# Both parts of a stationary float32r operand stored column by column in turn, in two transformer blocks on one core

## The chip, the cores and the metric

One Trainium2 chip, of which one core runs the kernel. The metric is device microseconds of one execution, the median of the runs shown. All inputs lie in the device's memory (DRAM) and are read from there in every execution.

## The reference, cut to what matters

Two transformer blocks of two layers each work one after the other on S = 256 tokens of width D = 1024 in float32. A layer of the first block is a mixer and a PEER layer; a layer of the second is a mixer (attention beside a Fourier mix) and a SwiGLU.

```python
# block 1, per layer
h = _modulate(x, sh1, sc1)
mix = _hybrid_mixer(h, ...)                 # projections, attention, conv, stick breaking, @ w_o
x = _layer_norm(ALPHA * x + (1 + g1) * mix, ...)
h = _modulate(x, sh2, sc2)
ffn = _peer(h, wq, sub_k1, sub_k2, U, V)    # per head the best 16 of 128 x 128 experts
x = _layer_norm(ALPHA * x + (1 + g2) * ffn, ...)
# _peer, per token: act = gelu(U[e] . h);  out = sum over e of g_e * act_e * V[e]
# block 2, per layer
p = h @ w_in                                # q, k, v, u
mix = concat([attention(q, k, v), fourier_mix(u)]) @ w_out
ffn = (silu(h @ w_gate) * (h @ w_up)) @ w_down   # hidden width 2816
```

The context stream of the second block has the same mixer and FFN in its first layer. What a float32 product needs of precision decides how it is made here (next section).

## The kernel before

**A product in three.** [...] So `split(dst_h, dst_l, src)` takes a float32 tile apart: ACT copies it, rounded, to `dst_h` (L261, "hi"), and DVE subtracts that from the source into `dst_l` (L263, "lo"). `mm3(o, lh, ll, rh, rl)` adds three products into one PSUM tile: lh x rh (L286), lh x rl (L287), ll x rh (L288). In each the first operand is the stationary one, which a weight load (LDWEIGHTS, shown as PEld) brings into the array, 128 columns of it; the second one is moving, and streams through, 256 or 512 columns. A load overlaps the matmul before it.

**Weights.** `wtile` starts the transfer of a raw weight tile of 512 KB on SP's queue (`raw_tile`, L256, five buffers), and splits it in two cuts. Each cut has a tile `wh` and a tile `wl`, two tags of the pool `ring` with five buffers (NHL) of 2048 B per partition each, so that hi and lo of one cut lie five buffers, 10,240 B, apart.

**Two kinds of products.**
- `gemm_t` (L290): the weight is stationary, [128 x 128] per k step; the activations (`hh`, `hl`, turned, 256 tokens) are the moving side. So are made the mixer projections of block 1 (`turned`: `sq`, `sk`, `cb`, `cc`, `ch`, L627), the PEER queries (`pwq`, L934), the expert inputs (`pact`, L958, the U stage), the projections of block 2 (`project`: `pw`) and the FFN's gate and up (`pwg`, `pwu`). Each weight tile is 8 k steps x 3 = 24 products of 256 columns.
- The products back to width 1024: the activations are stationary, 128 tokens by 128 channels, and the weights are the moving side, 512 columns. These are the expert outputs (`acc` with `WHL`, the V stage), the output projections of block 2 (`po`: stationary `mix`, or the FFN's `a` and `b`), and w_o of block 1 (`pm`: stationary `catH`, `catL`). For `pm` the split weights are `wok`, and for the last part of one `po` `kw`: both hold hi and lo in one tile [128, 2, 2, 512], 2048 B apart. `pn` (w1n) and `psc` have other stationaries.

**Stages of a PEER layer.** Queries and top-k with the first experts of the U stage beside them (layer 0: to some 415 us), the U stage with one-hot gate products `pG` (to 640 us), then the V stage (to 1005 us): there DVE multiplies the experts' activations by the gates (`Ws<-Ws,Gt`, L1024, which reads `Gt` with a step of 64 words), ACT and DVE split the product into `WHL`, and `acc` sums over 16,384 experts.

**Order.** A scheduler sorts the instructions of each engine from the program's order and its own costs; `Filler` generators put pieces of other work (top-k, gates, modulation products `adap` and `adac`) between the products, and `issue_after` pins some. One load of the kernel reads its stationary operand with a step of two words: `py` (L1321), where `uT` is read at every second token. The products of `adac` (L407) have a single moving column.

## Time and profile before

| | |
|---|---|
| median of 3 runs | 2874.16 us (2872.48 to 2876.75) |
| profiled execution | 2868.95 us, its span 2866.5 us |
| mean granted TensorE clock | 0.995 |
| TensorE busy / weight loads | 2802.3 us (98%) / 2436.2 us (85%) |
| DVE / ACT busy | 2204.3 us (77%) / 1673.2 us (58%) |
| read from and written to DRAM | 600.06 MB / 34.64 MB |

The span is the time from the first to the last instruction of the profiled execution; 2.45 us of that execution lie outside it. PE is TensorE's matmul, PEld its weight load, which runs beside matmuls. A matmul is pipelined: its own duration (279 ns for 256 columns, for instance) is longer than the distance from its start to the next start, so the busy share says only that something is in flight; the pace is read from counts in a stretch or from consecutive starts. [...] In names such as `pact<-hh,wh` the written tile stands left of the arrow, the read ones right.

### The profile page before, as it was taken

How to read it: one execution, taken by the hardware profiler on the slowest of the kernel's cores; microseconds unless marked ns; L12 is line 12 of the kernel's file. 1: busy time of each engine (PE TensorE's matmuls, PEld its weight loads, DVE VectorE, ACT ScalarE, POOL GpSimd, SP SyncE). 2: the span in 40 equal slices, each digit the busy share in tenths (PEclk: the TensorE clock that was granted, in tenths of full speed). 3: DMA queues.
4: the chain of work that ended last, by engine and by line, in shares of the span. 5: the costliest groups of instructions: out<-in, count | busy, mean ns of one | idle time of the engine just before them, and what ended most of it. 6: DMA issues, size and time to landing. Idle time of an engine off the chain costs nothing.

```text
span 2866.5 us, 53009 instructions
## 1 busy us (share of the span) xinstructions
PE 2802.3 (98%) x19114; PEld 2436.2 (85%) x19114; DVE 2204.3 (77%) x5110; ACT 1673.2 (58%) x3459; POOL 39.5 (1%) x50
## 2 busy tenths in 40 slices
PE   7999999999999999999999999999999999998999
PEld 4569999998888766899999888878769999887997
DVE  4469998987789767799888777888769766577565
ACT  3445568985555444555889655555556555566554
POOL 0000000000000000000000000000000000000000
PEclk9999999999999999999999999999999999999999
DMA  9775766667789867577666777976647665652454
GB/s 320 234 278 197 236 228 199 195 207 246 236 269 312 291 237 251 188 237 231 211 202 196 236 238 233 331 262 216 224 158 265 218 202 187 203 180 68 159 190 155
DMA packets 188112, 639.74 MB, mean 223 GB/s; under 512 B 22708, under 2 KB 24116, under 8 KB 187208
## 3 DMA queue, kind: packets, MB, share of 16 engines
q1 hardware_dynamic: 179208, 604.90, 63.9%
q10 hardware_dynamic: 8640, 31.46, 2.7%
q8 instruction: 149, 2.44, 0.3%
q14 instruction: 115, 0.94, 0.1%
HBM read 600.06 MB, written 34.64 MB: 221 GB/s over the span
## 4 chain that ended last, share of the span: by engine, by line
PE 92%; DVE 3%; DMA 2%; ACT 2%; issue 0%; POOL 0%; SPq 0%; DVEq 0%; POOLq 0%; ACTq 0%
PE pact L286 9%; PE pact L288 8%; PE pact L287 8%; PE acc L286 8%; PE acc L288 8%; PE acc L287 8%; PE po L286 3%; PE po L288 3%; PE po L287 3%; PE adap L340 2%; PE pwu L288 2%; PE pwu L287 2%; PE pwu L286 2%; PE pwg L286 2%; PE pwg L288 2%; PE pwg L287 2%
## 5 line engine op out<-in xcount | busy, mean ns | idle before, releaser
L261 ACT ACTIVATE wh<-raw 128x512 fp32r<-128x512 f32 (+1 forms) x1636 | 1010.0, 627 | 826.6 <-PE acc L288 289.8
L263 DVE TENSOR_TENSOR wl<-raw,wh 128x512 fp32r<-128x512 f32 (+1 forms) x1636 | 1094.2, 684 | 391.6 <-ACT wh L261 384.5
L286 PE MATMUL pact<-hh,wh 128*128 128x256 f32 x2048 | 583.0, 285 | 0.0
L288 PE MATMUL pact<-hh,wl 128*128 128x256 f32 x2048 | 572.3, 279 | 0.2 <-DVE wl L263 0.2
L287 PE MATMUL pact<-hl,wh 128*128 128x256 f32 x2048 | 571.4, 279 | 0.0
L286 PE MATMUL acc<-wh,WHL 128*128 128x512 f32 x1024 | 404.5, 396 | 1.2 <-ACT WHL L261 1.2
L288 PE MATMUL acc<-wh,WHL 128*128 128x512 f32 x1024 | 405.2, 396 | 0.0
L287 PE MATMUL acc<-wl,WHL 128*128 128x512 f32 x1024 | 405.1, 396 | 0.0
L287 PEld LDWEIGHTS pact<-hl,wh 128*128 128x128 f32 x2048 | 385.5, 188 | 0.0
L286 PEld LDWEIGHTS pact<-hh,wh 128*128 128x128 f32 x2048 | 385.3, 188 | 0.0
L288 PEld LDWEIGHTS pact<-hh,wl 128*128 128x128 f32 x2048 | 384.9, 188 | 0.4 <-DVE wl L263 0.4
L286 PEld LDWEIGHTS acc<-wh,WHL 128*128 128x128 f32 x1024 | 192.4, 188 | 50.2 <-ACT WHL L261 3.3
L287 PEld LDWEIGHTS acc<-wl,WHL 128*128 128x128 f32 x1024 | 192.4, 188 | 47.2 <-DVE WHL L263 0.9
L288 PEld LDWEIGHTS acc<-wh,WHL 128*128 128x128 f32 x1024 | 192.4, 188 | 47.1 <-DVE WHL L263 0.9
L985 ACT ACTIVATE hot<-hot,idxT 128x128 f16<-128x128 f16 x512 | 173.9, 401 | 1.3 <-DVE hot L984 1.2
L984 DVE TENSOR_SCALAR hot<-hot,idxT 128x128 f16<-128x128 f16 x512 | 158.6, 310 | 20.1 <-PE pG L986 19.8
L288 PE MATMUL pwu<-f,wl 128*128 128x256 f32 x512 | 143.1, 280 | 1.6 <-DVE wl L263 1.6
L286 PE MATMUL pwg<-f,wh 128*128 128x256 f32 x512 | 143.2, 280 | 0.0
L288 PE MATMUL pwg<-f,wl 128*128 128x256 f32 x512 | 143.0, 279 | 0.0
L287 PE MATMUL pwg<-f,wh 128*128 128x256 f32 x512 | 142.9, 279 | 0.0
L286 PE MATMUL pwu<-f,wh 128*128 128x256 f32 x512 | 142.9, 279 | 0.0
L287 PE MATMUL pwu<-f,wh 128*128 128x256 f32 x512 | 142.9, 279 | 0.0
(475 smaller groups left out, 5077.8 us busy)
## 6 DMA issues: line engine op xcount, KB each, us to landing
raw<-in_U_dram SPq DMA_DIRECT2D x256, 512.0 KB, 3.5
raw<-in_V_dram SPq DMA_DIRECT2D x256, 512.0 KB, 4.3
adaw<-in_ada_dram SPq DMA_DIRECT2D x192, 512.0 KB, 6.1
raw<-in_wg_dram SPq DMA_DIRECT2D x66, 512.0 KB, 3.5
raw<-in_wu_dram SPq DMA_DIRECT2D x66, 512.0 KB, 3.8
raw<-in_wd_dram SPq DMA_DIRECT2D x66, 512.0 KB, 3.3
spill<-gab ACTq DMA_DIRECT2D x60, 512.0 KB, 5.0
Ws<-spill SPq DMA_DIRECT2D x120, 256.0 KB, 3.9
```

The costliest lines, as they stand in the source:

```text
L261: SC.activation(dst_h, src, AF.Copy)
L263: return V.tensor_tensor(dst_l, src, dst_h, op=OP.subtract).ins
L286: T.matmul(o, lh, rh, start=first, stop=False)
L287: T.matmul(o, lh, rl, start=False, stop=False)
L288: T.matmul(o, ll, rh, start=False, stop=last)
L340: T.matmul(ps[32 * q:32 * q + 32, :], cvec(blk, k), r[h][:, 512 * (q % 2):512 * (q % 2) + 512], start=k == 0, stop=k == KB - 1, skip_group ...
L984: V.tensor_scalar(B, iota16, i2, g, op0=OP.is_equal, op1=OP.mult)
L985: SC.activation(B2, B, AF.Copy, scale=share)
```

## The change

Four things are done to layouts; the products and their order in the program stay as they are written.

- `pair` makes one tile with a last dimension of two, and returns its two views, so that a column's hi word and lo word are neighbours and each part is read and written with a step of two words (8 B). The stationary activations use it: `cat`, `WHL`, `mix`, `a`, `b`.
- `wtile(..., paired=True)` does the same for the weights of all `gemm_t` calls: tile `whl` [128, cut, 128, 2]. A load of 128 columns then reaches over 1024 B per partition in place of 512 B.
- The weights that are the moving side (V, `wo2`, `wd`) and `w1n` become one tile `whl` [128, 2, ...]: hi and lo, each contiguous, 2048 B apart, as in `wok` and `kw`.
- `turn_in` puts its `hh` and `hl` into one tile. Moving operands are contiguous as before. `ring` has one tag of five buffers of twice the size, so its size stays.

ACT writes, and DVE reads and writes, with a step of two words wherever a pair is split.

```diff
--- before.py
+++ after.py
@@ -256,6 +256,12 @@
         SP.dma_start(r, src)
         return r
 
+    def pair(p, n, cols, nm, tag=None):
+
+
+        t = p.tile([128, n, cols, 2], F32R, name=nm, tag=tag or nm)
+        return t[:, :, :, 0], t[:, :, :, 1]
+
     def split(dst_h, dst_l, src):
         with after(PIN.get("act")):
             SC.activation(dst_h, src, AF.Copy)
@@ -268,7 +274,7 @@
     def after(ins):
         return tc.issue_after(ins) if ins else ExitStack()
 
-    def wtile(src, shape, cuts=None, keep=None):
+    def wtile(src, shape, cuts=None, keep=None, paired=False):
 
 
         r = raw_tile(src, shape)
@@ -276,7 +282,12 @@
         c0 = 0
         for cut in cuts or [shape[0] // 2] * 2:
             sh = [cut] + shape[1:]
-            h, lo = [(keep or ring).tile([128] + sh, F32R, name=nm, tag=nm, bufs=4 if keep else NHL) for nm in ("wh", "wl")]
+            if paired:
+                t = ring.tile([128, cut, sh[1], 2], F32R, name="whl", tag="whl", bufs=NHL)
+                h, lo = t[:, :, :, 0], t[:, :, :, 1]
+            else:
+                t = (keep or ring).tile([128, 2] + sh, F32R, name="whl", tag="whl", bufs=4 if keep else NHL)
+                h, lo = t[:, 0], t[:, 1]
             LAST[0] = split(h, lo, r[:, c0:c0 + cut])
             parts.append((h, lo))
             c0 += cut
@@ -574,8 +585,7 @@
             SP.dma_start(cw, a["small1"][l])
             sh, sc = mod_cols(1, l, 0), mod_cols(1, l, 1)
             sth = ExitStack()
-            catH = p.tile([128, KB, S], F32R, name="catH")
-            catL = p.tile([128, KB, S], F32R, name="catL")
+            catH, catL = pair(p, KB, S, "cat")
             sbv = p.tile([128, 2, 256], F32, name="sbv")
             qln = p.tile([128, 2, 384], F32, name="qln")
             krn = p.tile([128, 2, 128], F32, name="krn")
@@ -624,7 +634,7 @@
                 i = 2 * order.index(nm)
                 ps = bank([128, 2, S], nm, "m")
                 for j in range(2):
-                    gemm_t(ps[:, j], wtile(a["w1t"][l, i + j], [KB, 128]), hh, hl, 0, S)
+                    gemm_t(ps[:, j], wtile(a["w1t"][l, i + j], [KB, 128], paired=True), hh, hl, 0, S)
                     ex.run(pace)
                 if nm in proj:
                     SC.activation(proj[nm], ps, AF.Copy)
@@ -931,7 +941,7 @@
                         pq = early[blk][1]
                     else:
                         pq = bank([128, S], "pwq", "a")
-                        gemm_t(pq, wtile(a["wq"][l, blk], [KB, 128]), hh, hl, 0, S)
+                        gemm_t(pq, wtile(a["wq"][l, blk], [KB, 128], paired=True), hh, hl, 0, S)
                     q = p.tile([128, S], F32, name="pqT", bufs=3)
                     SC.activation(q, pq, AF.Copy)
                     if prev:
@@ -955,7 +965,7 @@
                 ga = gab[:, j // 4 % 2]
                 ps = bank([128, 2, S], "pact", "a")
                 for c in range(2):
-                    gemm_t(ps[:, c], wtile(a["U"][l, j + c], [KB, 128]), hh, hl, 0, S)
+                    gemm_t(ps[:, c], wtile(a["U"][l, j + c], [KB, 128], paired=True), hh, hl, 0, S)
                     fl.run(budget / 2)
                 SC.activation(ga[:, j % 4:j % 4 + 2], ps, AF.Gelu)
                 if j % 4 == 2 and j < 120:
@@ -1004,7 +1014,7 @@
         stb.enter_context(banks(f"pb{l}", acc=2, m=3))
         acc = [bank([128, 2, 512], f"acc{tb}", "acc") for tb in range(2)]
         Ws = pa.tile([128, 4, 2, S], F32, name="Ws", tag="ha")
-        WHL = pa.tile([128, 2, 2, 2, S], F32R, name="WHL", tag="hb")
+        WHL = pair(pa, 4, S, "WHL", "hb")
         stl, stk = ExitStack(), ExitStack()
         held = {}
         last = None
@@ -1022,7 +1032,8 @@
                 spilled(j + 6)
             with tc.issue_after(last) if last else ExitStack():
                 V.tensor_tensor(W, W, Gt[j // 64][:, :, j % 64:j % 64 + 2].rearrange("p t j -> p j t"), op=OP.mult)
-            WH, WL = WHL[:, j // 2 % 2, 0], WHL[:, j // 2 % 2, 1]
+            b = 2 * (j // 2 % 2)
+            WH, WL = [part[:, b:b + 2] for part in WHL]
             last = split(WH, WL, W)
             late = j in order[-2:] and l == 0
             v = [wtile(a["V"][l, :, j + c, :], [1024], keep=kp if late and j == order[-1] else None) for c in range(2)]
@@ -1171,7 +1182,8 @@
                         tail(tb)
 
         def turn_in(p, s, cs, nm, bufs, px=None):
-            hh, hl = [p.tile([128, KB, S], F32R, name=f"{nm}{i}{s}", tag=f"{nm}{i}") for i in range(2)]
+            hp = p.tile([128, 2, KB, S], F32R, name=f"{nm}{s}", tag=nm)
+            hh, hl = hp[:, 0], hp[:, 1]
             for tb in range(2):
                 make_hT(px or p, xs[s][:, tb], "rms", cs[0], cs[1], hh, hl, 128 * tb, "m", bufs)
             return hh, hl
@@ -1192,7 +1204,7 @@
         mixT = {}
 
         def mix_tiles(s):
-            mixT[s] = [pm.tile([128, KB, S], F32R, name=f"mix{s}{i}", tag=f"mix{s}{i}") for i in range(2)]
+            mixT[s] = pair(pm, KB, S, f"mix{s}")
 
         stu = ExitStack()
         pq = stu.enter_context(pool(f"q{l}"))
@@ -1218,7 +1230,7 @@
             def project(b, hs):
 
 
-                w = wtile(a["w2t"][l, b], [KB, 128])
+                w = wtile(a["w2t"][l, b], [KB, 128], paired=True)
                 for s, (hh, hl) in hs.items():
                     ps = bank([128, 256], "pw2", "m")
                     gemm_t(ps, w, hh, hl, 0, S)
@@ -1454,7 +1466,7 @@
 
 
         fa1 = stp.enter_context(pool(f"ffa{l}"))
-        act[order[0]] = [fa1.tile([128, FB, S], F32R, name=f"a{i}") for i in range(2)]
+        act[order[0]] = pair(fa1, FB, S, "a")
         if both:
             fh0 = stp.enter_context(pool(f"ffg{l}"))
             sta = ExitStack()
@@ -1466,14 +1478,14 @@
                 ex.run()
                 stv.close()
                 fa0 = sta.enter_context(pool(f"ffb{l}", side="right"))
-                act[0] = [fa0.tile([128, FB, S], F32R, name=f"b{i}") for i in range(2)]
+                act[0] = pair(fa0, FB, S, "b")
             for f in range(FB):
                 if s:
                     ex.run(18.0 / (FB - 2))
                 pgu = [e[1] for e in early[2 * f:2 * f + 2]] if s == 0 else []
                 for nm in ("wg", "wu")[len(pgu):]:
                     pgu.append(bank([128, S], "p" + nm, "m"))
-                    gemm_t(pgu[-1], wtile(a[nm][l, f], [KB, 128]), *H[s], 0, S)
+                    gemm_t(pgu[-1], wtile(a[nm][l, f], [KB, 128], paired=True), *H[s], 0, S)
                 pg, pu = pgu
                 sg = fx.tile([128, S], F32, name="sg", bufs=2)
                 SC.activation(sg, pg, AF.Silu)
```

The number of instructions on each engine is the same before and after. Their order moves at few places. ACT, at the end of a block of queries in layer 0 (`wh`, `whl` are splits of weights, `pqT` copies of finished queries, `s` the scores' copies out of PSUM), the kernel before:

```order
L261 ACTIVATE wh<-raw 128x512 x2
L936 ACTIVATE pqT<-pwq 128x256
L261 ACTIVATE wh<-raw 128x512 x2
L936 ACTIVATE pqT<-pwq 128x256
L948 ACTIVATE s_1721<-pss_1795 128x512
L948 ACTIVATE s_1722<-pss_1796 128x512
L261 ACTIVATE wh<-raw 128x512 x2
L936 ACTIVATE pqT<-pwq 128x256
```

The two splits of the last weight stand behind both score copies. And the changed kernel, ACT at the same place:

```order
L267 ACTIVATE whl<-raw 128x512 x2
L946 ACTIVATE pqT<-pwq 128x256
L267 ACTIVATE whl<-raw 128x512 x2
L946 ACTIVATE pqT<-pwq 128x256
L267 ACTIVATE whl<-raw 128x512
L958 ACTIVATE s_1684<-pss_1756 128x512
L958 ACTIVATE s_1685<-pss_1757 128x512
L267 ACTIVATE whl<-raw 128x512
L946 ACTIVATE pqT<-pwq 128x256
```

Of the last weight before the next `pqT` one split now stands ahead of the two score copies and one behind them; before, both stood behind.

TensorE at the same place (`pss` are the score products, `pwq` the queries), the kernel before:

```order
L288 MATMUL pwq<-hh,wl 128x256
L921 MATMUL pss_1795<-pk,pqT 128x128
L921 MATMUL pss_1796<-pk,pqT 128x128
L286 MATMUL pwq<-hh,wh 128x256
L287 MATMUL pwq<-hl,wh 128x256
L288 MATMUL pwq<-hh,wl 128x256
L286 MATMUL pwq<-hh,wh 128x256
L921 MATMUL pss_1795<-pk,pqT 128x128
L921 MATMUL pss_1796<-pk,pqT 128x128
L287 MATMUL pwq<-hl,wh 128x256
L288 MATMUL pwq<-hh,wl 128x256
```

Four query products stand between the two pairs of score products. And the changed kernel, TensorE:

```order
L299 MATMUL pwq<-hh,whl 128x256
L931 MATMUL pss_1756<-pk,pqT 128x128
L931 MATMUL pss_1757<-pk,pqT 128x128
L297 MATMUL pwq<-hh,whl 128x256
L931 MATMUL pss_1756<-pk,pqT 128x128
L931 MATMUL pss_1757<-pk,pqT 128x128
L298 MATMUL pwq<-hl,whl 128x256
L299 MATMUL pwq<-hh,whl 128x256
L297 MATMUL pwq<-hh,whl 128x256
L298 MATMUL pwq<-hl,whl 128x256
```

The second pair of score products has moved ahead of a k step of the queries by three `pwq` products; all else stands as it stood.

## Rows read from the trace of the kernel before

**Rows 1.** The page: busy time of each engine, and the chain that ended last by engine.
```profile
PE 2802.3 (98%) x19114; PEld 2436.2 (85%) x19114; DVE 2204.3 (77%) x5110; ACT 1673.2 (58%) x3459; POOL 39.5 (1%) x50
PE 92%; DVE 3%; DMA 2%; ACT 2%; issue 0%; POOL 0%; SPq 0%; DVEq 0%; POOLq 0%; ACTq 0%
```

**Rows 2.** Windows: from:to, us, busy (x count) of PE, PEld, DVE, ACT, POOL, PEclk, DMA.
```profile
300.00:400.00 100.00, 100.00 (x860) 100.00 (x859) 94.64 (x238) 56.13 (x92) 0.00 (x0) 1.00 0.71 235
700.00:900.00 200.00, 200.00 (x858) 161.00 (x858) 160.96 (x226) 105.03 (x179) 0.00 (x0) 1.00 0.80 265
2654.50:2664.00 9.50, 9.50 (x44) 7.86 (x43) 4.09 (x7) 2.45 (x6) 0.55 (x1) 1.00 0.38 132
2200.00:2240.00 40.00, 40.00 (x345) 40.00 (x344) 33.88 (x52) 21.96 (x43) 0.00 (x0) 1.00 0.84 293
```

**Rows 3.** Groups by shape, TensorE's matmuls: busy us, mean ns of one | idle before.
```profile
L286 PE MATMUL pact<-hh,wh 128*128 128x256 f32 x2048 | 583.0, 285 | 0.0
...
L288 PE MATMUL acc<-wh,WHL 128*128 128x512 f32 x1024 | 405.2, 396 | 0.0
...
L288 PE MATMUL pwu<-f,wl 128*128 128x256 f32 x512 | 143.1, 280 | 1.6 <-DVE wl L263 1.6
...
L288 PE MATMUL po<-wh,a 128*128 128x512 f32 x176 | 69.6, 395 | 0.0
...
L288 PE MATMUL po<-wh,b 128*128 128x512 f32 x88 | 34.8, 396 | 0.0
...
L288 PE MATMUL po<-wh,mix 128*128 128x512 f32 x80 | 31.7, 396 | 0.0
...
L288 PE MATMUL po<-kw,mix 128*128 128x512 f32 x16 | 6.2, 389 | 0.0
```

**Rows 4.** Timeline, TensorE: start us, duration us, of `sq` in layer 1's mixer.
```profile
1043.80 0.28 PE L286 MATMUL sq<-hh,wh 128*128 128x256 f32 x1
...
1045.80 0.28 PE L288 MATMUL sq<-hh,wl 128*128 128x256 f32 x1
```

**Rows 5.** Timeline, TensorE: `cc` in the same mixer, 50 us later.
```profile
1094.96 0.28 PE L286 MATMUL cc<-hh,wh 128*128 128x256 f32 x1
...
1097.11 0.28 PE L287 MATMUL cc<-hl,wh 128*128 128x256 f32 x1
```

**Rows 6.** Timeline, TensorE: the projection of the last mixer with kept weights `kw`.
```profile
2657.79 0.39 PE L287 MATMUL po<-kw,mix 128*128 128x512 f32 x1
...
2659.38 0.39 PE L288 MATMUL po<-kw,mix 128*128 128x512 f32 x1
```

**Rows 7.** Groups by shape, TensorE's weight loads of 128 columns.
```profile
L286 PEld LDWEIGHTS pact<-hh,wh 128*128 128x128 f32 x2048 | 385.3, 188 | 0.0
...
L1333 PEld LDWEIGHTS pf<-k,Y 128*128 128x128 f32 x96 | 11.1, 192 | 0.3 <-ACT es L1366 0.2
...
L1321 PEld LDWEIGHTS py<-M,uT 128*128 128x128 f32 x48 | 9.0, 196 | 2.7 <-ACT PT L1385 1.7 <-ACT P L1370 0.2
```

**Rows 8.** Timeline, TensorE: 16 products with one moving column in a row.
```profile
938.99 1.84 PE L407 MATMUL adac<-k,adacc 128*128 128x1 f32 x16
```

**Rows 9.** Line 407: ns of its matmuls, lowest, median, highest; first and last start us.
```profile
L407 PE MATMUL adac<-k,adacc x48: 165/250/250, 939.0 to 2275.9; 128*128 128x1 f32 x48
```

**Rows 10.** Groups by shape, ACT: the split's first half.
```profile
L261 ACT ACTIVATE wh<-raw 128x512 fp32r<-128x512 f32 x1604 | 995.3, 630 | 797.6 <-PE acc L288 284.5 <-PE pact L287 139.5 <-PE po L288 89.6
```

**Rows 11.** Groups by shape, DVE: the split's second half, and the gating product.
```profile
L263 DVE TENSOR_TENSOR wl<-raw,wh 128x512 fp32r<-128x512 f32 x1604 | 1078.2, 687 | 382.2 <-ACT wh L261 375.8 <-PE sk L287 1.4 <-PE pw L288 1.4
...
L1024 DVE TENSOR_TENSOR Ws<-Ws,Gt 128x512 f32<-128x512 f32 x120 | 131.4, 1095 | 0.0
```

**Rows 12.** Windows of layer 0's stages: U with top-k, U with gates, V.
```profile
262.00:415.00 153.00, 152.82 (x1310) 152.62 (x1309) 145.42 (x392) 87.17 (x142) 0.00 (x0) 1.00 0.73 239
415.00:640.00 225.00, 225.00 (x2148) 222.09 (x2148) 199.53 (x684) 197.81 (x523) 0.00 (x0) 1.00 0.62 200
640.00:1005.00 365.00, 364.40 (x1571) 291.35 (x1573) 289.79 (x411) 189.23 (x323) 0.17 (x1) 1.00 0.81 269
```


## The prediction

> **What bounds the kernel now.** I read the page's totals first, then the chain, then stretches in which nothing but one kind of product runs. TensorE is busy for 98% of the span, and the chain that ended last lies on it for 92%, spread over the three lines of `mm3` [rows 1]. So the time is a number of matmuls times the distance from one start to the next, and the question is what sets that distance. The stretches answer it [rows 2]. [...] From 700 to 900 us, in the V stage, 858 of 512 columns: 233.1 ns. The FFN's gate and up products, 2200 to 2240 us, give 345 in 40 us, again 116 ns. TensorE shows no idle time there, so no wait sets this pace. [...]
>
> The pace is not the same everywhere. The products of `sq` at 1043.80 to 1045.80 us make 17 steps in 2.00 us, 117.6 ns [rows 4]; those of `cc` at 1094.96 to 1097.11 us, the same code with the same moving tiles, make 19 steps in 2.15 us, 113.2 ns [rows 5]. Among the 512-column products `po<-kw,mix` is the exception: from 2654.5 to 2664 us there are 44 in 9.50 us [rows 2], a pace that its starts from 2657.79 to 2659.38 us, 7 steps in 1.59, give exactly [rows 6], and one lasts 389 ns, while `po<-wh,mix` with the same stationary tile lasts 396 and the other products of the kind 395 to 396 [rows 3]. What differs is where the moving parts lie: `kw` keeps hi and lo in one tile, 2048 B apart, the ring's `wh` and `wl` are two tags 10,240 B apart. So there are two paces, 233.3 and 226.7, 116.7 and 113.3, and an identical product can run at either, depending on how its operands meet in the memory. That is what this change touches.
>
> **The change part by part.** No instruction is added or removed; matmuls, loads, splits and transfers keep their number, and the few places where the order changes are single splits and half k steps. At the end of a query block ACT now takes one split ahead of the two copies of `s`, which come later by it, and TensorE makes the second pair of `pss` three products, 0.35 us, earlier. I cost the order at nothing: who waits for `s` is the top-k on DVE, and TensorE has expert products queued that need none of it; without that cover it would be one split, 0.63 us [rows 10], at some 16 block ends, at most 10 us.
>
> *Merged halves for the 512-column products.* V, wo2 and wd tiles become one tile with hi and lo 2048 B apart, which is the layout of `kw`. `acc` has 3 x 1024 products, `po` from the ring 3 x (176 + 88 + 80) [rows 3], together 4104. The nearest row is `kw` itself: 226.7 in place of 233.3, 6.67 ns x 4104 = **-27 us**. [...] I take -27, the row that has this moving layout.
>
> *Stationary operands read at every second word.* All `gemm_t` weights, 256-column products: `pact` 3 x 2048 and `pwg`, `pwu` 3 x 1024 [rows 3], 9216, and by the loops of the code another 1,872 (`pwq` 624, `project` 768, mixer 480), together 11,088. Two things can happen. The load can become longer. One load in the kernel before already reads every second word: `py<-M,uT`, 196 ns, against 192 for `pf<-k,Y` right behind it and 188 for `pact` [rows 7]. So +4 to +8 ns. What a load costs when it alone sets the pace is seen at `adac`, with one moving column: 16 in 1.84 us [rows 8], of which the last lasts between 0.165 and 0.250 [rows 9], so 106 to 112 ns each; since 112 is below 116.7, loads are just hidden today, with some 5 ns to spare. If the 4 to 8 ns are a delay at its start, they vanish in the overlap; if they are pace, loads come every 116 to 120 ns and are level with the matmuls or above. Or the load can get out of the moving stream's way, and the products fall to the short pace that `cc` shows: 3.33 ns x 11,088 = **-37 us**. The ends are (120 - 116.7) x 11,088 = +37 us (the 8 ns whole as pace) and -52 us (down to 112, where today's loads would bind). I take -37: the short pace is a row of this very product, and the load's extra 4 ns, if it is delay, stays below the 113.3.
>
> *The splits write and read every second word.* Each of ACT's copies writes with a step of 8 B, each of DVE's subtractions reads one operand and writes one with that step. No row shows an engine doing this. DVE's split of a weight takes 687 ns, ACT's 630 [rows 10, 11]; the nearest row with a stepped operand is `Ws<-Ws,Gt`, which reads with a step of 64 words and takes 1095 ns, 408 more than a contiguous one. I take 687 unchanged, since a step of two is nearest to none; the bounds are 687 and 1095. What covers it: in the U stage with top-k, 262 to 415 us, DVE is busy 145.42 of 153 us [rows 12]. 1310 matmuls / 24 per weight x 2 halves = 109 splits, so 7.58 / 109 = 70 ns each are free: up to 757 ns the stride is free, above it DVE sets the end. From 415 to 640 us it has 25.5 us over some 136 splits, 187 ns each. In the V stage, 640 to 1005 us, only one split in five is strided, and DVE has 75 us. The shorter pace itself takes 1310 x 3.33 = 4.4 us of the 7.58, so it just fits.
>
> [...] The row shows a stepped load 4 ns longer than the plain one beside it [rows 7]. [...]
>
> **Sum.** -27 - 37 = -64 us. The profiled execution is 2868.95 us (span 2866.5 and 2.45 outside it), 5.2 us below the median of 2874.16; against it the sum is 2805, against the median **2810 us**, which is my forecast.
>
> **Rivals.**
> 1. *Only the merged tiles act* (the pace hangs on the moving layout, and `gemm_t`'s moving tiles `hh`, `hl` of block 1 stay as they were): -27, 2847. For: in `po` only the moving side differs between the two paces. Against: `sq` and `cc` differ with no layout changed at all. Chance 0.13.
> 2. [...] Chance 0.12. [...]
> 3. *Nothing moves.* [...] Chance 0.17.
> 4. *The stepped load becomes the bound* of the 256-column products. It decides from 116.7 ns, a load longer by 5 in pace; at 118.5 to 120 it costs 1.8 to 3.3 ns x 11,088 = +20 to +37: 2894 to 2911. Where the merged tiles act too it is 27 less, and the change comes out slower only from some 119.5. For: loads fill the U stage without a gap (100.00 of 100 us) [rows 2], with 5 to 11 ns between their own pace and the matmuls'. Against: the single stepped row is only 4 ns longer. Chance 0.20. Slower.
> 5. *DVE becomes the bound* in the U stage, from 757 ns per split. At 1095: 109 x 0.408 - 7.6 = 37 us, and 136 x 0.408 - 25.5 = 30, each in two layers: +134, up to 3008; at 850, 109 x 0.163 - 7.6 = 10, twice: +20. Chance 0.08. Slower.
>
> **How the numbers follow.** The forecast itself, both kinds at the short pace, has 0.30. Cases that are faster by more than 0.2% (5.7 us, about what a measurement of this kernel can tell from no change): 0.30 + 0.13 + 0.12 = 0.55. Same: 0.17. Slower: 0.20 + 0.08 = 0.28. The faster cases alone span 2740 to 2850. The range that should hold 8 in 10 takes in these, "nothing moves" and most of rival 4 and leaves out its far end and most of rival 5, some 0.14 together: 2740 to 2905.
>
> **What would show it.** Short pace: 300 to 400 us holds 882 matmuls in place of 860, `acc` lasts about 389 ns and its starts lie 227 ns apart. Merged only: `acc` falls, `pact` stays at 116.7. [...] Load bound: `pact` loads without a gap and starts above 116.7, while `po` and `acc` keep or better theirs. DVE: the group of weight splits above 757 ns and TensorE waiting for it in the U stage. The sum is wrong if the `pact` loads come back longer by more than 5 ns per start, or if the pace of `acc` does not follow that of `kw`.

## The result and the profile after

The changed kernel takes 2912.34 us in the median of 4 runs (2906.18 to 2914.77), the kernel before 2875.45 us (4 runs too, one more than above): a ratio of 1.0126, 95% interval 1.0107 to 1.0145, so it is 1.3% slower. The forecast was 2810, the range ended at 2905.

The page of the changed kernel, busy time of each engine and the chain by engine, to stand beside [rows 1]; then its windows, with the columns of [rows 2] (us; busy and count of PE, PEld, DVE, ACT, POOL; PEclk, the granted clock, 1.00 its full speed; DMA share; GB/s):

```profile
span 2904.4 us, 52798 instructions
PE 2843.4 (98%) x19114; PEld 2514.4 (87%) x19114; DVE 2212.3 (76%) x5110; ACT 1714.6 (59%) x3459; POOL 38.4 (1%) x50
PE 92%; DMA 3%; DVE 3%; ACT 2%; issue 0%; SPq 0%; POOL 0%; DVEq 0%; POOLq 0%; ACTq 0%
```

```profile
300.00:400.00 100.00, 100.00 (x829) 100.00 (x829) 92.68 (x235) 58.13 (x90) 0.00 (x0) 1.00 0.70 223
700.00:900.00 200.00, 200.00 (x864) 168.74 (x863) 160.11 (x226) 106.45 (x180) 0.00 (x0) 1.00 0.80 262
262.00:415.00 153.00, 153.00 (x1267) 153.00 (x1267) 143.23 (x379) 87.63 (x135) 0.00 (x0) 1.00 0.71 230
```

TensorE is still busy without a gap, at the same granted clock of 1.00, and gets through fewer products: 829 of 256 columns in 100 us where 860 stood, 120.6 ns each in place of 116.3. The V stage is a little faster: 864 in 200 us, 231.5 ns in place of 233.1. DVE isn't the bound: TensorE and its loads wait for nothing in the U stage (153.00 of 153 us each), while DVE is busy for 143.23 us there, 145.42 before [rows 12]. Groups by shape of the changed kernel, weight loads, the splits on ACT and DVE, and three products:

```profile
L298 PEld LDWEIGHTS pact<-hl,whl 128*128 128x128 f32 x2048 | 404.2, 197 | 0.0
...
L299 PEld LDWEIGHTS acc<-whl,WHL 128*128 128x128 f32 x1024 | 200.6, 196 | 37.8 <-DVE WHL L269 0.8
...
L1333 PEld LDWEIGHTS py<-M,uT 128*128 128x128 f32 x48 | 9.0, 196 | 2.6 <-ACT PT L1397 1.7 <-ACT P L1382 0.2
```

```profile
L267 ACT ACTIVATE whl<-raw 128x512 fp32r<-128x512 f32 x1604 | 1034.2, 657 | 666.2 <-PE acc L299 279.8 <-PE pact L299 103.5 <-PE po L299 88.6
```

```profile
L269 DVE TENSOR_TENSOR whl<-raw,whl 128x512 fp32r<-128x512 f32 x1604 | 1080.4, 689 | 406.7 <-ACT whl L267 403.3
```

```profile
L299 PE MATMUL acc<-whl,WHL 128*128 128x512 f32 x1024 | 404.0, 395 | 0.0
...
L299 PE MATMUL pm<-wok,cat 128*128 128x512 f32 x64 | 25.2, 394 | 0.0
...
L299 PE MATMUL po<-kw,mix 128*128 128x512 f32 x16 | 6.3, 395 | 0.0
```

The loads of `pact` and `acc` now last as long as that of `py`, 196 to 197 ns against 188 [rows 7]. The splits' groups mix stepped and contiguous weights: DVE 689 ns (687 before), ACT 657 (630). From 415 to 640 us all weights are stepped; there ACT's copies take 672 ns in place of 626 (before, then after), DVE's subtractions 688 in place of 686:

```profile
L261 ACT ACTIVATE wh<-raw 128x512 fp32r<-128x512 f32 x137 | 82.4, 626 | 10.2 <-PE pact L287 9.4 <-ACT wh L261 0.8
```

```profile
L267 ACT ACTIVATE whl<-raw 128x512 fp32r<-128x512 f32 x132 | 83.1, 672 | 3.4 <-DVE whl L269 1.4 <-PE pact L299 1.0 <-PE pG L996 0.7
```

And `po<-kw,mix`, the row that my first term rested on, has gone the wrong way, from 389 ns to 395. By the two windows the sum is +4.3 ns x 11,088 = +48 us for the 256-column products and -1.6 x 4104 = -7 for the others, +41 together, near the 37.9 by which the spans differ. A window's count takes in the products under way at its start and a few of other kinds. By the starts of all neighbouring products of a trace (steps across another product or a missing record left out) `pact` goes from 116.9 to 120.7 ns and `acc` from 233.3 to 232.1: +3.8 x 11,088 = +42 and -1.2 x 4104 = -5, together +37.

### The profile page after: what moved, and what is told of

It reads as the page before. It is cut to its first block, busy times and chain, and to the rows that moved or that the text cites. A ratio compares the mean times of both kernels' runs of the same rounds, so it can differ in the third digit from the quotient of the medians.

```text
span 2904.4 us, 52798 instructions
## 1 busy us (share of the span) xinstructions
PE 2843.4 (98%) x19114; PEld 2514.4 (87%) x19114; DVE 2212.3 (76%) x5110; ACT 1714.6 (59%) x3459; POOL 38.4 (1%) x50
## 4 chain that ended last, share of the span: by engine, by line
PE 92%; DMA 3%; DVE 3%; ACT 2%; issue 0%; SPq 0%; POOL 0%; DVEq 0%; POOLq 0%; ACTq 0%
PE pact L297 9%; PE pact L298 9%; PE pact L299 8%; PE acc L297 8%; PE acc L299 8%; PE acc L298 8%; PE adap L351 3%; PE po L297 3%; PE po L298 2%; PE po L299 2%; PE pwu L299 2%; PE pwu L298 2%; PE pwu L297 2%; PE pwg L297 2%; PE pwg L299 2%; PE pwg L298 2%
## 5 line engine op out<-in xcount | busy, mean ns | idle before, releaser
L267 ACT ACTIVATE whl<-raw 128x512 fp32r<-128x512 f32 (+1 forms) x1636 | 1048.8, 654 | 694.7 <-PE acc L299 285.4
L269 DVE TENSOR_TENSOR whl<-raw,whl 128x512 fp32r<-128x512 f32 (+1 forms) x1636 | 1096.5, 685 | 415.9 <-ACT whl L267 411.9
L297 PE MATMUL pact<-hh,whl 128*128 128x256 f32 x2048 | 594.3, 290 | 0.0
L298 PE MATMUL pact<-hl,whl 128*128 128x256 f32 x2048 | 584.5, 285 | 0.0
L299 PE MATMUL pact<-hh,whl 128*128 128x256 f32 x2048 | 581.9, 284 | 0.0
L297 PE MATMUL acc<-whl,WHL 128*128 128x512 f32 x1024 | 403.4, 395 | 1.3 <-ACT WHL L267 1.3
L298 PEld LDWEIGHTS pact<-hl,whl 128*128 128x128 f32 x2048 | 404.2, 197 | 0.0
L298 PE MATMUL acc<-whl,WHL 128*128 128x512 f32 x1024 | 404.0, 395 | 0.0
L299 PE MATMUL acc<-whl,WHL 128*128 128x512 f32 x1024 | 404.0, 395 | 0.0
L297 PEld LDWEIGHTS pact<-hh,whl 128*128 128x128 f32 x2048 | 403.7, 197 | 0.0
L299 PEld LDWEIGHTS pact<-hh,whl 128*128 128x128 f32 x2048 | 403.4, 197 | 0.0
L297 PEld LDWEIGHTS acc<-whl,WHL 128*128 128x128 f32 x1024 | 200.5, 196 | 41.1 <-ACT WHL L267 3.4
L299 PEld LDWEIGHTS acc<-whl,WHL 128*128 128x128 f32 x1024 | 200.6, 196 | 37.8 <-DVE WHL L269 0.8
L298 PEld LDWEIGHTS acc<-whl,WHL 128*128 128x128 f32 x1024 | 200.6, 196 | 37.6 <-DVE WHL L269 0.9
L299 PE MATMUL pwu<-f,whl 128*128 128x256 f32 x512 | 145.8, 285 | 1.5 <-DVE whl L269 1.5
L297 PE MATMUL pwg<-f,whl 128*128 128x256 f32 x512 | 145.9, 285 | 0.0
L299 PE MATMUL pwg<-f,whl 128*128 128x256 f32 x512 | 145.6, 284 | 0.0
L298 PE MATMUL pwg<-f,whl 128*128 128x256 f32 x512 | 145.6, 284 | 0.0
L298 PE MATMUL pwu<-f,whl 128*128 128x256 f32 x512 | 145.5, 284 | 0.0
L297 PE MATMUL pwu<-f,whl 128*128 128x256 f32 x512 | 145.5, 284 | 0.0
```

The costliest lines, as they stand in the source:

```text
L267: SC.activation(dst_h, src, AF.Copy)
L269: return V.tensor_tensor(dst_l, src, dst_h, op=OP.subtract).ins
L297: T.matmul(o, lh, rh, start=first, stop=False)
L298: T.matmul(o, lh, rl, start=False, stop=False)
L299: T.matmul(o, ll, rh, start=False, stop=last)
```

## The experiments

Two questions were open: which part of the change makes the 256-column products slower, and what sets the two paces that the kernel before shows. The theory (A) is that a load at a step of two words is itself too slow to hide. Its rivals are (B) the stepped splits on ACT and DVE and (C) the merged tiles.

### The change taken apart: weights, activations, merging alone

e1, against the changed kernel: the activations are contiguous, the weights of `gemm_t` stay stepped.

```diff
     def pair(p, n, cols, nm, tag=None):
-        t = p.tile([128, n, cols, 2], F32R, name=nm, tag=tag or nm)
-        return t[:, :, :, 0], t[:, :, :, 1]
+        t = p.tile([128, 2, n, cols], F32R, name=nm, tag=tag or nm)
+        return t[:, 0], t[:, 1]
```

> Only the weights of the 256-column products alternate hi and lo; the stationary activations hold their two halves one behind the other, 2048 B or more apart. Theory A, the stepped load is itself the slower one: pact loads 197 ns, 829 products from 300 to 400 us as in the changed kernel, 4.0 ns x 11,088 = +44 us against the kernel before, less what the merged 512-column tiles bring (0 to 27). Theory B, the time goes to the splits' stepped writes and reads on ACT and DVE: the same time as the changed kernel, but by waits of TensorE for splits. Rival C, the merged tiles cost it and not the step: no more than +10 us here with loads of 188 ns.

e2 leaves `pair` as it is and takes `paired=True` away from all five calls of `wtile`:

```diff
-    gemm_t(..., wtile(a["U"][l, j + c], [KB, 128], paired=True), hh, hl, 0, S)
+    gemm_t(..., wtile(a["U"][l, j + c], [KB, 128]), hh, hl, 0, S)
```

> Only the stationary activations of the 512-column products alternate hi and lo; the weights of the 256-column products hold two contiguous halves in one tile. Theory A: acc loads 196 ns, but hidden under 232 ns: acc starts 231 to 233 ns apart, pact back at 116.7 with loads of 188, in all -5 to 0 us against the kernel before; and pm with kept w_o goes from 227 to 233 ns as in the changed kernel. If instead the step is a help to 512-column products, acc comes down to 227 or less: -27 us.

e3 does both, so that only the merging of hi and lo into one tile is left.

> Nothing alternates; only hi and lo halves are in one tile, contiguous, 2048 B apart (wtile, turn_in) or one half apart (activations). If the short pace of kw and w_o belongs to the moving layout with plain loads: acc and po from the ring at 226.7 ns, -27 us against the kernel before, and pact at 116.7 or 113.3. If that pace is a matter of address or phase: the time of the kernel before within 6 us.

Measured against the kernel before: e1 2912.28 us, ratio 1.0137 (1.0119 to 1.0154); e2 2871.81, 0.9999 (0.9989 to 1.0009); e3 2875.07, 1.0009 (0.9998 to 1.0019). The whole loss comes with the stepped weights. The first three fences are windows of e1, e2 and e3, U stage and V stage; the last two are the load of `pact` and the split on ACT in e2:

```profile
300.00:400.00 100.00, 100.00 (x830) 100.00 (x829) 92.11 (x231) 57.76 (x89) 0.00 (x0) 1.00 0.70 227
700.00:900.00 200.00, 200.00 (x858) 160.99 (x857) 158.12 (x224) 105.24 (x179) 0.00 (x0) 1.00 0.79 259
```

```profile
300.00:400.00 100.00, 100.00 (x859) 100.00 (x859) 95.35 (x245) 56.24 (x92) 0.00 (x0) 1.00 0.72 232
700.00:900.00 200.00, 200.00 (x863) 168.44 (x863) 160.83 (x227) 106.88 (x180) 0.00 (x0) 1.00 0.81 265
```

```profile
300.00:400.00 100.00, 100.00 (x852) 100.00 (x851) 94.58 (x236) 55.46 (x92) 0.00 (x0) 1.00 0.73 229
700.00:900.00 200.00, 199.51 (x855) 160.14 (x854) 157.04 (x221) 104.59 (x178) 0.00 (x0) 1.00 0.80 258
```

```profile
L298 PEld LDWEIGHTS pact<-hl,whl 128*128 128x128 f32 x2048 | 385.7, 188 | 0.0
```

```profile
L267 ACT ACTIVATE whl<-raw 128x512 fp32r<-128x512 f32 x1604 | 990.2, 629 | 667.2 <-PE acc L299 277.8 <-PE pact L299 105.8 <-PE po L299 89.0
```

e1 has the 830 products of the changed kernel in 100 us, e2 the 859 of the kernel before; e3 has 852 in this window, but 117.1 ns for `pact` by all starts, as e2 has 116.9. The stepped activations bring the small gain of the V stage (863 in 200 us); with `pm` and `kw` slower it is worth some 3 us by the paces, at the edge of what e2's interval can tell. C falls with e3; the merged layout does not give `acc` the pace of `kw` either: `acc` stays at 233 ns there (855 in 200 us), with nothing stepped. e1 alone can't tell A from B, since weights that are read at a step are also split at one. The trace of the changed kernel can: between two starts of `pact` lie 120.7 ns on average where no split of a weight runs on ACT or DVE (1022 steps), and 120.8 where one runs on both for nearly all of the time (542 steps). In the kernel before these are 117.1 and 116.8. The loss is there whether a split runs beside the products or not, and TensorE has no idle time in the U stage; B falls.

### Loads without splits beside them

The probes leave the reference's work out: they load a few weights and run chains of products on a core whose other engines are idle, so only the pace of a chain counts. The first has this core, in which `one`, `two`, `four` are stationary tiles with a step of 1, 2, 4 words, `m256` and `mnear`, `mfar` moving tiles of 256 and 512 columns, the latter two with hi and lo 2048 or 10,240 B apart; the single loads behind the chains belong to plain float32 products:

```python
for i in range(n):
    mm3(ps[:, :cols], *st[i % len(st)], *mv[i % len(mv)], i == 0, i == n - 1)
```

> A probe without the reference's work: it loads some weights, splits nothing, and runs chains of 96 float32r products in triples as in mm3, one chain behind another, with no other engine at work, and 48 float32 products with one moving column for stationary steps of 1, 2 and 4 words. Theory A: the chain qone (256 columns, contiguous) at about 116.7 ns from start to start, qtwo (step 2) at about 120.6, qfour (step 4) at 120.6 or more; the one-column products 112 at step 1 and 117 to 121 at step 2, more at step 4. Theory B (writes beside it): qone and qtwo the same. For 512 columns: rnearone 226.7 and rfarone 233.3 if the moving layout sets the pace; both the same if it does not; rneartwo and rfartwo about 232 as in the changed kernel.

Timeline of this probe (start us, duration us), first and last rows of stretches of four chains: 85 steps of `qfour`, 86 of `rnearone` and 85 of `rneartwo`, and 84 of `qtwo` ahead of them:

```profile
52.13 0.28 PE L286 MATMUL qtwo<-hh,ctwo 128*128 128x256 f32 x1
...
62.21 0.28 PE L286 MATMUL qtwo<-hh,ctwo 128*128 128x256 f32 x1
...
63.65 0.39 PE L286 MATMUL qfour<-hh,cfour 128*128 128x256 f32 x1
...
83.48 0.40 PE L287 MATMUL qfour<-hl,cfour 128*128 128x256 f32 x1
...
107.83 0.39 PE L286 MATMUL rnearone<-vhl,cone 128*128 128x512 f32 x1
...
127.33 0.39 PE L288 MATMUL rnearone<-vhl,cone 128*128 128x512 f32 x1
...
152.00 0.39 PE L286 MATMUL rneartwo<-vhl,ctwo 128*128 128x512 f32 x1
...
171.83 0.39 PE L287 MATMUL rneartwo<-vhl,ctwo 128*128 128x512 f32 x1
```

`qtwo` makes 10.08 / 84 = 120.0 ns with no split anywhere: near the pace of the changed kernel. `qfour` needs 19.83 / 85 = 233 ns, twice that. With 512 columns a contiguous load allows 19.50 / 86 = 226.7, a stepped one 233.3, so there the step can cost too. `rfarone` and `rnearone` had the same pace, 226.7: how far apart the moving halves lie made no difference there. But `qone`, contiguous, also ran at 120.0, not at the 116.9 that `pact` has in the kernel before. That was the outcome named for B, so this probe by itself does not speak for A; and the step was not the only thing that sets the pace. What differed, by the addresses that the allocator gives, is the place of the operands: in the probe both start at the same place within 64 bytes, in the kernel before `pact` and `acc` have them 32 bytes apart, and `kw` and `wok`, the fast ones, 0. While the single loads of this probe ran, with one moving column each, the granted clock fell to 0.5; from there on step 1 and step 2 both took 213 ns.

The second probe moves the stationary start by 8 bytes from chain to chain, and repeats the single loads behind a chain of 512-column products.

```python
run("q%s%s" % ("xy"[rnd], n), one(w), m256, 16, 256)      # w words into the stationary tile
...
T.matmul(ps[:, i:i + 1], rr[:, o:o + 128 * step:step], rr[:, 7:8], start=True, stop=True)
```

> A second probe without the reference's work: chains of 48 float32r products, no other engine at work, in which the first byte of the stationary operand moves against that of the moving one: 0, 8, 16 ... 56 bytes (letters a to h), each for 256 columns (q) and 512 columns (r), up (x) and down (y); then stationary operands with a step of two words at 0 and 32 bytes (tq, tr), and 20 float32 products with one moving column with step 1 (lone) and 2 (ltwo) behind a warm chain. If the start of the operands within 64 bytes sets the pace: ra 226.7 ns and re 233.3, as w_o and kw (both starts equal) against acc and po from the ring (32 bytes apart), and q chains between 113 and 120 by letter. If it does not: all r alike, all q alike. Theory A for the step: ltwo 117 to 121 ns at the upper clock where lone has 112.

Timeline of the second probe: 40 loads with one moving column, contiguous and at a step of two, at a granted clock of 1.00.

```profile
312.01 4.52 PE L1548 MATMUL lonea<-raw 128*128 128x1 f32 x40
...
329.00 4.76 PE L1548 MATMUL ltwoa<-raw 128*128 128x1 f32 x40
```

This is the price by itself, at that clock: (4.76 - 4.52) / 39 = 6.2 ns more per load. Once settled their starts lie 111.7 and 117.8 ns apart. 111.7 hides under the 116.9 of `pact`; 117.8 does not. By this a 256-column product with a stepped load does not come at the old pace; the fourth probe bears it out for float32r. But it accounts for no more than 117.8 - 116.9 = 0.9 of the 3.8 ns. The offsets did matter: `q` ran at 115.5 to 123 ns and `r` at 226.7 to 233.5 by letter, both rounds alike but for two letters (16 bytes: `r` at 233.3 and 226.7; 48 bytes: `q` at 117.8 and 123.0).

The fourth probe asks why the changed kernel has 120.6 rather than 117.8: it runs stepped chains at 32 distances.

> The third probe again, without the reference's work, but with stationary operands at a step of two words; letters a to z, A to F are distances of 0 to 248 bytes between the starts. If the stepped load is the bound by itself (117.8 ns in the second probe): all q chains at 117.8 or a little above, whatever the letter. If it joins the other two streams in a fixed pattern: q at 120.0 at all or nearly all letters, with none at 113 to 117. If the distance matters as much as with contiguous loads: q from 117.8 up to 124, and a better place for the changed kernel would be among the letters.

First and last row of two of its `q` chains, 47 steps each, at 80 and 224 bytes:

```profile
195.44 0.28 PE L286 MATMUL qk<-hh,ctwo 128*128 128x256 f32 x1
...
200.98 0.28 PE L288 MATMUL qk<-hh,ctwo 128*128 128x256 f32 x1
...
500.02 0.28 PE L286 MATMUL qC<-hh,ctwo 128*128 128x256 f32 x1
...
505.66 0.28 PE L288 MATMUL qC<-hh,ctwo 128*128 128x256 f32 x1
```

At 80 bytes 5.54 / 47 = 117.9 ns, the lowest of the 32; at 224, where `pact` stands, 5.64 / 47 = 120.0; the highest some 123. Most of the 32, 18 of them, settle at 119.9 to 120.1. No chain goes below the pace of the single load, and a stepped load seldom reaches it beside a moving stream. At 224 bytes the contiguous chain of the third probe (next section) takes 5.54 / 47 = 117.9:

```profile
496.56 0.28 PE L286 MATMUL qC<-hh,cone 128*128 128x256 f32 x1
...
502.10 0.28 PE L288 MATMUL qC<-hh,cone 128*128 128x256 f32 x1
```

The step alone, with no split and no other engine at work, costs 2.1 ns there. So A is shown in kind, a stepped load costs the 256-column products their pace; why it is 120.0 so often, and 3.8 ns rather than 2.1 in the kernel, stays open.

### The place of the operands

The third probe walks the contiguous chains through 256 bytes.

> A third probe without the reference's work: chains of 48 float32r products with contiguous operands, no other engine at work; the start of the stationary operand moves against that of the moving one by 8 bytes from chain to chain, 0 to 248 bytes (letters a to z, A to F), for 256 (q) and 512 columns (r). If only the distance of the two starts within 256 bytes sets the pace: ra 226.7 ns and nearly all others 230 to 233.3, with 226.7 again at no other letter or at 16 bytes alone, where one of two earlier chains had it; q at 224 bytes (letter C), where pact stands, 116.7 ns as in the kernel before, at 0 about 120, at 32 bytes about 118.4. If the two states are a matter of phase: letters scatter without order between 113 and 120, and 226.7 and 233.3.

Timeline of the third probe, first and last rows: `r` at 0 (45 steps shown) and 32 bytes (47), `q` at 168 (47):

```profile
32.69 0.40 PE L288 MATMUL ra<-vhl,cone 128*128 128x512 f32 x1
...
42.91 0.39 PE L288 MATMUL ra<-vhl,cone 128*128 128x512 f32 x1
...
98.23 0.40 PE L286 MATMUL re<-vhl,cone 128*128 128x512 f32 x1
...
109.20 0.40 PE L288 MATMUL re<-vhl,cone 128*128 128x512 f32 x1
...
379.35 0.28 PE L286 MATMUL qv<-hh,cone 128*128 128x256 f32 x1
...
384.69 0.28 PE L288 MATMUL qv<-hh,cone 128*128 128x256 f32 x1
```

`r` at 0 bytes makes 227 ns, at 32 bytes 233.4, with 226.7 again only at 120 and 240 bytes. `q` has 113.3 once it has settled at 168 bytes, 115.6 at 8, 117.8 at 224, and 116.7 to 120 elsewhere, in no order that I can state. The other `r` chains take 229 to 234.3. The letters of the second probe came back with the same values, the two doubtful ones with one of their two. So the pace changes with the two addresses, and mostly repeats. The distance is not all, for 256 columns: in the kernel before `sq` and `cc` have one distance by the allocator, 192 bytes, and `cc` itself has both paces. Its first weight tile makes 23 steps in 2.71 us, 117.8 ns, where its second made 113.2 [rows 5]:

```profile
1086.21 0.28 PE L286 MATMUL cc<-hh,wh 128*128 128x256 f32 x1
...
1088.92 0.28 PE L288 MATMUL cc<-hh,wl 128*128 128x256 f32 x1
```

The "matter of phase" of the third probe's expectation is not excluded there.

e5 tested this in the kernel. Against e3, the stationary activations begin 32 bytes later:

```diff
+        t = p.tile([128, 2 * n * cols + 16], F32R, name=nm, tag=tag or nm)
+        t = t[:, 8:8 + 2 * n * cols].rearrange("p (i n c) -> p i n c", i=2, n=n)
```

> As e3 (nothing alternates), but the stationary activations WHL, mix, a and b begin 32 bytes later, so that they and the moving weights start at the same place within 64 bytes; for w_o and kw the two, equal before, are then 32 bytes apart. If the start within 64 bytes sets the pace of 512-column products: acc and po from the ring at 226.7 ns, 4104 x 6.67 = -27 us against the kernel before, pm and po from kw at 233.3 (+1.6 us). If it is the pool or the region of memory: the time of e3, paces as there.

It took 2867.46 us, ratio 0.9983 (0.9974 to 0.9992): -5, where -27 was expected. The gain came only in part, and was given back in part. Windows of e5, and its groups of `acc` and of `po` from `a` and from `b`:

```profile
300.00:400.00 100.00, 100.00 (x847) 100.00 (x847) 93.99 (x242) 55.68 (x91) 0.00 (x0) 1.00 0.69 230
700.00:900.00 200.00, 199.33 (x876) 163.73 (x875) 159.66 (x227) 106.80 (x183) 0.00 (x0) 1.00 0.80 265
```

```profile
L300 PE MATMUL acc<-whl,WHL 128*128 128x512 f32 x1024 | 398.8, 389 | 0.0
...
L300 PE MATMUL po<-whl,a 128*128 128x512 f32 x176 | 69.6, 395 | 0.0
...
L300 PE MATMUL po<-whl,b 128*128 128x512 f32 x88 | 34.2, 389 | 0.0
```

The V stage has the short pace (876 in 200 us). But the larger tiles moved what lies behind them by 64 bytes, so `pact` changed its distance too, from 224 to 32 bytes (847 in 100 us in place of 860), and `po` from `a` and `mix` stayed at 233: within 64 bytes their starts agreed, within 256 they did not, while for `acc` and for `po` from `b`, both near 226.7, they did. The unit is 256 bytes, as far as these tiles tell. `pm` and `po` from `kw` went to 233 as expected.

e6 keeps that in order: tiles of 256 bytes more, a start 224 bytes later, for `WHL`, `a` and `b` only; `pact` keeps its distance.

```diff
+        n = int(np.prod(shape))
+        t = p.tile([128, n + 64], F32R, name=nm, tag=tag)[:, words:words + n]     # words = 56
```

> As e3 (nothing alternates), but WHL, a and b start 224 bytes later within tiles that are 256 bytes longer, so that for acc and for po from a and b the stationary and the moving operand start at the same place within 256 bytes (before: 32 bytes apart), while the 256-column products keep their distance of 224 bytes. If that distance sets the pace: acc and po from a and b at 226.7 ns, pact at 116.7 as before: (3072 + 528 + 264) x 6.67 = -26 us against the kernel before. In e5 pact had moved to a distance of 32 bytes and lost some 1.3 ns x 6768 = 9 us and more again; if e5's small gain has another reason, e6 gives no more than e5, -5 us.

It took 2853.23 us (2851.26 to 2854.27), ratio 0.9932 (0.9919 to 0.9946): faster than both kernels, by 18 us against the one before. Windows and the group of `acc` in e6:

```profile
300.00:400.00 100.00, 100.00 (x860) 100.00 (x859) 95.45 (x237) 55.82 (x92) 0.00 (x0) 1.00 0.72 234
700.00:900.00 200.00, 199.24 (x878) 164.34 (x877) 161.72 (x230) 106.74 (x182) 0.00 (x0) 1.00 0.79 270
...
640.00:1005.00 365.00, 360.87 (x1609) 292.90 (x1610) 292.93 (x419) 189.34 (x324) 1.46 (x1) 1.00 0.80 275
```

```profile
L305 PE MATMUL acc<-whl,WHL 128*128 128x512 f32 x1024 | 398.8, 389 | 0.0
```

`acc` lasts 389 ns and `pact` is where it was. Of the 26 us some 8 are missing; a part of them is idle time that the faster V stage lets show: TensorE stands still for 4.13 of 365 us there, against 0.60 before [rows 12].

e7 and e8 tried the two good distances of the probe on the 256-column products as well; they move `hh`, `hl` of PEER and FFN by 56 and by 216 bytes, and to make room they give one temporary of the projections two buffers in place of three. The lines of PEER:

```diff
-        hh = pa.tile([128, KB, S], F32R, name="hh", tag="ha")
-        hl = pa.tile([128, KB, S], F32R, name="hl", tag="hb")
+        hh = at(pa, [KB, S], "hh", "ha", 14)     # words; e8: 54
+        hl = at(pa, [KB, S], "hl", "hb", 14)
```

> As e6, and the moving hh, hl of the PEER stages and those of the FFN start 56 bytes later, so that pact, pwq, pwg and pwu have the distance of 168 bytes at which a chain of the third probe ran at 113.33 ns; one temporary of the projections (sb) has two buffers in place of three to make room. If the distance alone sets the pace also beside other engines: 9840 products x 3.4 = -33 us against e6, -59 against the kernel before. If the 113.33 of the probe holds only in a quiet chain: pact at 116 to 120, 0 to +33 us against e6.

> As e7, but hh, hl of PEER and FFN start 216 bytes later, a distance of 8 bytes, at which two probes gave 115.5 to 115.6 ns. If the place of the starts carries over from the quiet chain: pact, pwq, pwg, pwu at 115.6, 9840 x 1.0 = -10 us against e6, -28 against the kernel before. If not, as with 168 bytes: pact at 117 to 120, +4 to +33 us against e6.

Both lost, to the kernel before and by 25 us and more to e6: e7 2882.12 us, 1.0036 (1.0022 to 1.0049); e8 2878.22, 1.0023 (1.0014 to 1.0033). The U stage of e7, then that of e8, and a load in e7:

```profile
300.00:400.00 100.00, 100.00 (x835) 100.00 (x835) 93.08 (x234) 54.59 (x90) 0.00 (x0) 1.00 0.68 224
```

```profile
300.00:400.00 100.00, 100.00 (x836) 100.00 (x835) 93.03 (x234) 55.21 (x91) 0.00 (x0) 1.00 0.67 224
```

```profile
L304 PEld LDWEIGHTS pact<-hl,whl 128*128 128x128 f32 x2048 | 391.3, 191 | 0.0
```

119.8 and 119.6 ns by these counts, 120.2 and 120.0 by the starts, where the quiet chains had 113.3 and 115.6, with contiguous loads that last 191 ns in e7. So a distance that is best in a chain alone need not be so in the kernel, and for 256 columns the distance bears on the pace but the probe does not say which is good. What else in the kernel decides it was not tried.

## Why the prediction was wrong

**What bounds the kernel: right.** The time is products times pace, and the result is a change of pace: by the starts +3.8 ns in the one kind and -1.2 in the other.

**Merged halves, -27 us: wrong; merging alone brings nothing (e3), the change as a whole -5 for these products.** I chose the row of `kw` as "the row that has this moving layout". It has that layout and the short pace, but it also had both operands at the same start, as `wok` had. e3 gave the layout without the pace, e6 the pace by the start alone with the same layout. I had two operands whose places I could have worked out, and compared only one.

**Stepped loads, -37 us: wrong in sign; it is +48 by the window, +42 by the starts.** The step that failed is the choice between "delay" and "pace" for the extra 4 to 8 ns. I had set the load's own pace (106 to 112 ns) against the matmuls' 116.7, and seen that 5 ns were to spare; then I took the gain of `cc`, a pace that needs loads below 113.3, for an edit that by `py` makes loads longer (196 ns against 188 to 192). Measured, the load costs 6.2 ns in pace and stands at 117.8, above the products' own pace; beside a moving stream it costs more than this floor, 120.0 in the quiet chain and 120.7 in the kernel, and that part has no explanation here. `py` could not show it, since its own matmul of 379 ns covers a load of 196 wholly. There was no row for the gain either: `sq` and `cc` differ with no step in either.

**The step and the place, by the runs.** The single loads take 111.7 ns at step 1 and 117.8 at step 2, 5.5% more, and a 256-column chain at step 4 goes at 233. `rnearone` and `rneartwo` differ only in the step of a load (188 and 193 ns long) that 512 columns cover, and go at 226.7 and 233.3 ns; in e6 the place of one operand alone changes the pace of `acc` by 6.5 ns, from e3's 233.3 to 226.9. So in these two chains a load shorter than the product beside it still bore on that product's pace.

**Splits: right.** 689 ns on DVE, far from the 757 from which it decides; ACT's 46 ns more for a stepped copy lie under its idle time. **Order at nothing:** e2 and e3, which were scheduled anew too, come out at the time of the kernel before; it wasn't tested apart.

**The rivals.** Rival 4 is what happened: "it decides from 116.7 ns, a load longer by 5 in pace", 2894 to 2911. The median is 1 us beyond its end; against the kernel before it is +36.9 us, the upper end of rival 4. I gave it 0.20 for a single row with 4 ns; the row of the load's own pace, 112 against 116.7, was the better ground, and by it the chance of a gain for the 256-column products was small. Rival 1 fell with e3. The lower end of the range, 2740 us, and the chance of 0.12 take 512-column products some 20 ns closer together than 233.3, an estimate of mine that no run shows; the shortest pace that the runs showed for them is 226.7. The pace of the U stage hangs on the load and on the place of the operands, and the change touched only the first, for the worse.

## What to carry to other kernels

When loads run without a gap, their own pace (here 111.7 ns contiguous, 117.8 at a step of two) is the figure to set against the matmuls' (here 116.9) before an edit that touches them: products with one moving column showed it here. Look for the pace of like products at other places in the same trace; where two exist, compare the addresses of both operands, not only the one that the edit moves. For 512-column float32r products, starting the stationary and the moving operand at the same place within 256 bytes was worth some 6.5 ns each here, and a pad that does it must not move the others.

## What the runs showed of the hardware

- A load of 128 float32 columns at a step of two words costs 6.2 ns more in pace than a contiguous one at a granted clock of 1.00 (117.8 against 111.7); at 0.5 both took 213 ns. At a step of four a chain of 256-column products goes at 233 ns.
- The pace of float32r products with contiguous loads changes with where the two operands start against each other. For 512 columns it is 226.7 to 234.3 ns in a quiet chain, and in the kernel some 227 with equal starts and 233 at 32 bytes. For 256 columns it is 113.3 to 123 in a quiet chain and 116.9 to 120.2 for `pact` in the kernel, and there the distance is not all: `cc` has 113.2 and 117.8 at one distance.
- DVE's subtraction with a step of two words in one operand and in the result took 688 ns for 512 columns, the contiguous one 686; ACT's copy with a stepped result 672 against 626 (415 to 640 us, after and before).
